# Adding loads for two sums of each weight block, and the down projection's operands kept in DRAM

## The chip, the cores and the metric

The kernel runs on one core of one Trainium2 chip. A time is the device time of one execution in microseconds (us). TensorE (PE) multiplies matrices, with its weight loads (PEld) beside it; VectorE (DVE) and ScalarE (ACT) work elementwise; GpSimd (POOL) does so too and issues DMAs of its own, whose descriptors are made by software; SyncE (SP) issues nearly all other DMAs. Every engine, and every queue of DMA issues, runs its instructions in the order in which the program holds them. An instruction that waits holds up all that stand behind it on its engine.

## What is computed

One layer of a streaming encoder on 576 tokens (512 of a new stream, 64 of a running one): layer norm, a mixer (RWKV-7 and S5), an output projection with a second layer norm, a SwiGLU feed-forward part with a third. The change touches the feed-forward part alone:

```python
def swiglu(x, w1, w3, w2):
    return (jax.nn.silu(x @ w1) * (x @ w3)) @ w2

x = layer_norm(ALPHA * x + mix, ln1_g[l], ln1_b[l])
x = layer_norm(ALPHA * x + swiglu(x, ffn_w1[l], ffn_w3[l], ffn_w2[l]), ln2_g[l], ln2_b[l])
```

The model width is 2048 and the hidden width 5632; all arrays are float32.

## The kernel before

Activations stand transposed: features on the 128 partitions, 576 tokens along the free axis, in two halves of 288. Every float32 operand is split in a high and a low part (`wh`, `wl` for weights), and each product is three matmuls (high-high, high-low, low-high) of 128x128 weights on 128x288 activations.

The feed-forward part multiplies by a Strassen-Winograd scheme. A block pair of weights is a 2x2 arrangement of 128-column blocks of four 128-row tiles each. Seven products do the work of eight, but need sums of blocks: `s1` (product 5), `s2` (product 6), `s3` (product 7), and a changed block for product 3.

`stationary` (L1470) makes the seven weight operands of one call. It loads a raw tile `fr` of 128x8x256 with two DMAs from SP (L1475; the pool `fraw` holds two such tiles), forms `s1` and `s2` on DVE, `s3` (L1484) and the block of product 3 (L1497) on POOL, and for each product casts the high part on ACT (`S.copy(wh, x)`, L1493) and subtracts it on DVE (`wl`, L103). The pool `wsp` has three buffers each for `wh` and `wl`, so at most three products stand ready ahead of PE.

`up` (L1511) is one pair of output blocks of `w1` or `w3`: two calls of `stationary` (q = 0, 1), each followed by 7 x 12 matmuls (`product`, L1505), then eight combinations of the seven PSUM banks into `c` (one copy on ACT, seven additions on DVE through `e` and `f`). The loop over 22 pairs runs `up(w1)`, Silu on ACT, `up(w3)`, the product of both on POOL (L1537) and two stores to the DRAM tensor `gd` (L1538): four calls of `stationary` a pair, 88 in all.

The down projection takes 40 row blocks in five chunks of eight. `moving` (L1554) loads four blocks `g` of a chunk, forms the three sums and the seven operands `gq` from them (DVE, ACT, and POOL in pieces of 128x288), and for each of the eight pairs of output blocks a call of `stationary(w2, ...)` and 7 x 12 matmuls follow (L1614), with results added into `acd` (`fold` on DVE, three additions on POOL). Four row blocks that are left over are done at the end without the scheme.

The order of work is set by a scheduler: `high_priority(offset=250)` around `stationary`, `offset=600` around `moving`. It places instructions by a modelled time, and what it wrote down is then fixed for each engine.

Of the kernel before, what the change touches and what calls it, by code (L numbers as in the profile page):

```python
# [8 lines left out]
F32 = mybir.dt.float32  # L9
# [3 lines left out]
ALU = mybir.AluOpType  # L13
# [4 lines left out]
P = 128  # L18
# [42 lines left out]
def tile_hybrid_step(ctx: ExitStack, tc: tile.TileContext, a, o, dbg=None):  # L61
# [1346 lines left out]
    rps = stats.rstd(pv)  # L1410
    mean = stats.mean()
# [14 lines left out]
    for kh in range(2):  # L1426
        ks = slice(4 * kh, 4 * kh + 4)

        def norm(j, h):
            q = acc[j][:, h, ks]  # L1430
            ts = slice(h * HF, (h + 1) * HF)
            tt(q, q, bcm(mean[:, ts], 4), ALU.subtract)
            tt(q, q, bcm(rstd[:, ts], 4), ALU.mult)
            for k in range(4):
                m = 8 * j + 4 * kh + k
                S.activation(q[:, k], q[:, k], AF.Identity, bias=par["ln1_b"][:, m:m + 1],
                             scale=par["ln1_g"][:, m:m + 1])
# [9 lines left out]
        tt(b11, b12, b11, ALU.subtract)  # L1447
# [19 lines left out]
    def bank(n=HF):  # L1467
        return pd.tile([P, 512], F32, tag="pb", name="pb")[:, :n]

    def stationary(src, r1, r2, col, order):  # L1470


        raw = fraw.tile([P, 8, 256], F32, tag="fr", name="fr")
        for i, r in enumerate((r1, r2)):
            nc.sync.dma_start(raw[:, 4 * i:4 * i + 4], src[r:r + 512, col:col + 256].rearrange("(k p) c -> p k c", p=P))  # L1475
        blk = {(i, j): raw[:, 4 * j:4 * j + 4, i * P:i * P + P] for i in range(2) for j in range(2)}

        def s_(nm):
            return wraw.tile([P, 512], F32, tag="raw", name=nm).rearrange("p (k c) -> p k c", c=P)

        ops, out = {1: blk[0, 0], 2: blk[0, 1], 4: blk[1, 1]}, {}
        s1, s2, s3 = s_("s1"), s_("s2"), s_("s3")
# [3 lines left out]
        ops[5], ops[6], ops[7] = s1, s2, s3  # L1486
# [12 lines left out]

    def product(ps, w, x, first, last):  # L1500
# [10 lines left out]
    def up(src, col):  # L1511

        ps = {n_: bank() for n_ in UP}
        for q in range(2):
            with tc.high_priority(offset=250):
                ws = stationary(src, 512 * q, 1024 + 512 * q, col, UP)
# [15 lines left out]
    for m in range(0, DFF // P, 2):
        sg = up(w1, m * P)
        for x in sg:
            S.activation(x, x, AF.Silu)
# [9 lines left out]
    def operand():  # L1545
# [5 lines left out]
        place.append(room[-1][:, n % 2])  # L1551
        return place[-1]

    def moving(ck):  # L1554

        g = big2.tile([P, 2, 2, 4, HF], F32, tag="big2", name="g")
        for j in range(2):
            r0 = (8 * ck + 4 * j) * P
            for h in range(2):
                nc.sync.dma_start(g[:, j, h], gd[r0:r0 + 4 * P, h * HF:h * HF + HF].rearrange("(k p) n -> p k n", p=P))  # L1560
        b = {(j, h): g[:, j, h] for j in range(2) for h in range(2)}
        out = {}

        def sp(n_, q):
# [4 lines left out]
        sp(1, b[0, 0])  # L1569
        sp(2, b[1, 0])  # L1570
        tt(b[0, 0], b[0, 1], b[0, 0], ALU.subtract)
        t2 = t2_("t2"), t2_("t2")
        t2 = [x for t_ in t2 for x in hs(t_)]
        for k in range(4):
            G.tensor_tensor(t2[k], b[1, 1][:, k], b[0, 0][:, k], ALU.subtract)
        out[6] = operand()
        for k in range(4):
            S.copy(out[6][:, 0, k], t2[k])
            tt(out[6][:, 1, k], t2[k], out[6][:, 0, k].bitcast(F32), ALU.subtract)
            G.tensor_tensor(b[1, 0][:, k], b[1, 0][:, k], t2[k], ALU.subtract)  # L1580
        sp(5, b[0, 0])
        tt(b[0, 1], b[1, 1], b[0, 1], ALU.subtract)
        sp(7, b[0, 1])
        sp(3, b[1, 1])
        sp(4, b[1, 0])
# [6 lines left out]
    def fold(d_, ps, ck):  # L1592
        if ck == 0:
            stt(d_, d_, ALPHA, ps, ALU.mult, ALU.add)
        else:
            tt(d_, ps, d_, ALU.add)

    for ck in range(NCK):
        with tc.high_priority(offset=600):
            gq = moving(ck)  # L1600
        for m in range(0, 16, 2):
            with tc.high_priority(offset=250):
                ws = stationary(w2, 1024 * ck, 1024 * ck + 512, m * P, DOWN)
            c1, c2 = (hs(acc[m // 8][:, m % 8 + i]) for i in range(2))
            pa, pb_, pc = bank(), bank(), bank()
            e, f = hs(w5("e")), hs(w5("f"))
            for n_ in DOWN:
                ps, first, last = {1: (pa, True, False), 2: (pb_, True, True), 6: (pa, False, False), 5: (pc, True, False),
                                   7: (pa, False, False), 3: (pc, False, True), 4: (pa, False, True)}[n_]
                x = gq[n_]  # L1610
                n = 0
                for k in range(4):
                    for w_, x_ in ((ws[n_][0], x[:, 0]), (ws[n_][0], x[:, 1]), (ws[n_][1], x[:, 0])):
                        T.matmul(ps, w_[:, k], x_[:, k], start=first and n == 0, stop=n == 11, skip_group_check=True)  # L1614
                        n += 1
                if n_ == 1:
                    S.copy(e[0], pa)
                elif n_ == 2:
                    fold(c1[0], pb_, ck)
                    G.tensor_tensor(c1[0], c1[0], e[0], ALU.add)  # L1620
                elif n_ == 6:
                    S.copy(e[1], pa)
                elif n_ == 5:
                    fold(c2[1], pc, ck)
                elif n_ == 7:
                    S.copy(f[0], pa)
                    G.tensor_tensor(c2[1], c2[1], f[0], ALU.add)
                elif n_ == 3:
                    fold(c1[1], pc, ck)
                    G.tensor_tensor(c1[1], c1[1], e[1], ALU.add)  # L1630
                else:
                    fold(c2[0], pa, ck)


    NB = 4
# [93 lines left out]
```

## Time and profile before

| | |
|---|---|
| median of 3 runs | 2833.76 us (2829.86 to 2834.14) |
| the profiled execution | 2835.99 us |
| its span, first to last instruction | 2834.1 us |
| PE busy | 2648.2 us (93%) |
| DVE busy | 2177.8 us (77%) |
| ACT busy | 1286.4 us (45%) |
| POOL busy | 683.3 us (24%) |
| DMA, mean | 119 GB/s |
| up part, first to last matmul of L1505 | 1165.5 to 2203.6 us |
| down part, five chunks, L1614 | 2203.9 to 2745.1 us |

Times in the trace count from the first instruction. A PE that is busy is not PE at its peak, since matmuls overlap; how fast they follow each other is read from the starts in the timeline. A row of the timeline has start, duration, engine, line, operation, operands, count, and in brackets how long the engine had been idle and what ended that.

### The profile page before, as it was taken

The page shows a single profiled execution, that of the slowest core. Times are in us where ns is not written, and L with a number is a line of the kernel's source. Part 1 is how long each engine was busy: PE and PEld are TensorE (multiplying, and loading weights), DVE is VectorE, ACT ScalarE, POOL GpSimd, SP SyncE. Part 2 cuts the span into 40 slices and gives each one's busy share as a digit, 9 for nine tenths or more (in the row PEclk, how much of TensorE's full clock was granted, in tenths as well). Part 3 has the DMA queues.
Part 4 walks back from the last instruction along what each step waited for, and adds up shares of the span by engine and source line. Part 5 has one row for each costly group of instructions (what it writes and reads, how often), then busy time and mean ns, then how long its engine had stood idle before and what let it go on. Part 6 is the DMA issues. An engine that isn't in the chain of part 4 may idle for free. (4 is left out here: it accounts for less than half of the span.)

```text
span 2834.1 us, 55090 instructions
## 1 busy us (share of the span) xinstructions
PE 2648.2 (93%) x21280; PEld 2511.0 (89%) x21280; DVE 2177.8 (77%) x4011; ACT 1286.4 (45%) x2535; POOL 683.3 (24%) x609
## 2 busy tenths in 40 slices
PE   6999999999999999499999999999999799899896
PEld 4999998888788889399999999999999788799895
DVE  5768856768786456877777777777777998988888
ACT  5344434455665432544444444444434443444443
POOL 0010000000000000033232333323332656554530
PEclk8999999999999999699999999999999899999998
DMA  6456756433434352233333333333333432332334
GB/s 189 131 134 197 216 174 179 119 99 98 126 78 116 93 152 71 82 132 107 98 107 103 115 104 102 106 99 111 109 105 102 167 108 90 100 117 90 117 99 137
DMA packets 422908, 338.50 MB, mean 119 GB/s; under 512 B 87362, under 2 KB 388532, under 8 KB 421556
## 3 DMA queue, kind: packets, MB, share of 16 engines
q1 hardware_dynamic: 421940, 332.80, 38.5%
q8 instruction: 167, 2.74, 0.4%
q10 hardware_dynamic: 288, 2.10, 0.2%
q14 instruction: 97, 0.79, 0.1%
q0 software_dynamic: 416, 0.07, 0.0%
HBM read 271.11 MB, written 63.79 MB: 118 GB/s over the span
## 5 line engine op out<-in xcount | busy, mean ns | idle before, releaser
L1505 PE MATMUL pb<-xq,wh 128*128 128x288 f32 x4928 | 994.1, 297 | 23.0 <-ACT xq L1417 16.0
L1505 PEld LDWEIGHTS pb<-xq,wh 128*128 128x128 f32 x4928 | 795.1, 189 | 25.4 <-ACT xq L1417 17.3
L1505 PE MATMUL pb<-xq,wl 128*128 128x288 f32 x2464 | 730.7, 297 | 18.5 <-DVE wl L103 18.1
L1493 ACT CAST wh<-fr 128x512 fp32r<-128x512 f32 x512 | 317.7, 621 | 518.1 <-PE pb L1505 338.3
L1614 PE MATMUL pb<-gq,wh 128*128 128x288 f32 x2240 | 462.3, 304 | 36.0 <-DVE acd L103 12.0
L1505 PEld LDWEIGHTS pb<-xq,wl 128*128 128x128 f32 x2464 | 467.0, 190 | 25.3 <-DVE wl L103 25.3
L103 DVE TENSOR_TENSOR wl<-s,wh 128x512 fp32r<-128x512 f32 x384 | 421.5, 1105 | 49.6 <-ACT wh L1493 43.9
L103 DVE TENSOR_TENSOR wl<-fr,wh 128x512 fp32r<-128x512 f32 x512 | 362.2, 715 | 74.9 <-ACT wh L1493 68.3
L1614 PEld LDWEIGHTS pb<-gq,wh 128*128 128x128 f32 x2240 | 368.2, 195 | 47.0 <-DVE acd L103 12.3
L1493 ACT CAST wh<-s 128x512 fp32r<-128x512 f32 x384 | 238.4, 621 | 330.5 <-PE pb L1505 165.3
L1614 PE MATMUL pb<-gq,wl 128*128 128x288 f32 x1120 | 330.8, 306 | 19.2 <-DVE wl L103 18.2
L129 PE MATMUL pb<-xh,wh 128*128 128x288 f32 x1120 | 338.4, 304 | 2.9 <-ACT pbuf L366 2.1
L129 PE MATMUL pb<-xl,wh 128*128 128x288 f32 x1120 | 338.9, 304 | 0.0
L129 PE MATMUL pb<-xh,wl 128*128 128x288 f32 x1120 | 338.0, 304 | 0.5 <-DVE wl L103 0.5
L1484 POOL TENSOR_TENSOR s<-fr 128x512 f32<-128x512 f32 x128 | 185.6, 1450 | 466.9 <-DVE wl L103 448.8
L103 DVE TENSOR_TENSOR wl<-raw,wh 128x512 fp32r<-128x512 f32 x252 | 173.6, 689 | 134.9 <-ACT wh L301 132.6
L301 ACT CAST wh<-raw 128x512 fp32r<-128x512 f32 x252 | 156.2, 620 | 242.7 <-PE pb L129 184.1
L1497 POOL TENSOR_TENSOR fr<-fr,s 128x512 f32<-128x512 f32 x128 | 172.3, 1346 | 370.7 <-DVE wl L103 370.7
L1614 PEld LDWEIGHTS pb<-gq,wl 128*128 128x128 f32 x1120 | 214.7, 195 | 26.8 <-DVE wl L103 26.6
L129 PEld LDWEIGHTS pb<-xh,wh 128*128 128x128 f32 x1120 | 212.4, 190 | 9.3 <-ACT pbuf L366 2.5
L129 PEld LDWEIGHTS pb<-xh,wl 128*128 128x128 f32 x1120 | 211.8, 190 | 7.9 <-DVE wl L103 1.4
L129 PEld LDWEIGHTS pb<-xl,wh 128*128 128x128 f32 x1120 | 212.5, 190 | 4.8 <-issue 0.2
(498 smaller groups left out, 4200.4 us busy)
## 6 DMA issues: line engine op xcount, KB each, us to landing
fr<-in_ffn_w_dram SPq DMA_DIRECT2D x256, 512.0 KB
raw<-in_w_in_dram SPq DMA_DIRECT2D x140, 256.0 KB
raw<-in_w_out_dram SPq DMA_DIRECT2D x64, 256.0 KB
gd<-c SPq DMA_DIRECT2D x44, 288.0 KB
g<-gd SPq DMA_DIRECT2D x20, 576.0 KB
raw<-in_ffn_w_dram SPq DMA_DIRECT2D x32, 256.0 KB
lwd<-low SPq DMA_DIRECT2D x24, 288.0 KB
rkd<-psh SPq DMA_DIRECT2D x24, 288.0 KB
```

Source lines behind the costliest of these rows:

```text
L103: V.tensor_tensor(out, x, y, op)
L129: T.matmul(out, w, x, **kw)
L301: S.copy(wh, raw)
L1484: G.tensor_tensor(s3, blk[0, 0], blk[1, 0], ALU.subtract)
L1493: S.copy(wh, x)
L1497: G.tensor_tensor(blk[0, 1], blk[0, 1], s2, ALU.subtract)
L1505: T.matmul(ps, w_[:, k], x_[:, k], start=first and n == 0, stop=last and n == 11)
L1614: T.matmul(ps, w_[:, k], x_[:, k], start=first and n == 0, stop=n == 11, skip_group_check=True)
```

## The change

**Loads.** `stationary` no longer has one raw tile. It has four, each with two buffers: `a11` and `a2` (both blocks of the second row half in one tile) are plain loads, and `s1` and `s3` are made in two steps: a plain load of one block from SP, and a second load from POOL's queue that adds another block to what stands in the tile (`accum_op=ALU.add`). `s2` and the block of product 3 stay sums of two tiles, both now on DVE. Signs are turned so that the two loaded sums are additions; the operands of the activations, Silu and the folds carry the signs.

**Product of the two halves.** The two gate products move from POOL to DVE.

**Down operands.** For 20 of 22 pairs DVE forms four more tiles of 128x288 (`n1`, `t3`, `n2`, `n4`), and seven stores a pair go to a DRAM tensor `gp`, in place of two to `gd`. `moving` loads each operand ready-made into a quarter of one staging tile `stg` and only splits it.

```diff
-    def stationary(src, r1, r2, col, order):
-        raw = fraw.tile([P, 8, 256], F32, tag="fr", name="fr")
-        for i, r in enumerate((r1, r2)):
-            nc.sync.dma_start(raw[:, 4 * i:4 * i + 4], src[r:r + 512, col:col + 256].rearrange("(k p) c -> p k c", p=P))
...
-        tt(s1, blk[1, 0], blk[1, 1], ALU.add)
-        G.tensor_tensor(s3, blk[0, 0], blk[1, 0], ALU.subtract)
-        tt(s2, s1, blk[0, 0], ALU.subtract)
+    def stationary(halves, col, order):
+        def rows(i, j, n=1):
+            return halves[j][:, :, col + i * P:col + (i + n) * P]
+        def t_(nm):
+            return fraw.tile([P, 4, P], F32, tag=nm, name=nm)
+        a11, s1, s3 = t_("a11"), t_("s1"), t_("s3")
+        a2 = fraw.tile([P, 4, 2 * P], F32, tag="a2", name="a2")
+        nc.sync.dma_start(a11, rows(0, 0))
+        nc.sync.dma_start(s1, rows(1, 0))
+        nc.sync.dma_start(s3, rows(0, 0))
+        nc.gpsimd.dma_start(s1, rows(1, 1), accum_op=ALU.add)
+        nc.gpsimd.dma_start(s3, rows(1, 0), accum_op=ALU.add)
+        nc.sync.dma_start(a2, rows(0, 1, 2))
...
         for n_ in order:
-            if n_ == 3:
-                ops[3] = blk[0, 1]
+            if n_ == 6:
+                tt(s2, s1, a11, ALU.add)
+                tt(a12, a12, s2, ALU.add)
...
-            if n_ == 2:
-                G.tensor_tensor(blk[0, 1], blk[0, 1], s2, ALU.subtract)
...
-        for i, (x, y) in enumerate(zip(sg, up(w3, m * P))):
-            G.tensor_tensor(y, x, y, ALU.mult)
-            nc.sync.dma_start(gd[(m + i) * P:(m + i + 1) * P], y)
+        g = up(w3, 2 * i * P)
+        tt(g[0], sg[0], g[0], ALU.mult)
+        stt(g[1], g[1], -1.0, sg[1], ALU.mult, ALU.mult)
...
+        tt(n1, b11, b12, ALU.subtract)
+        tt(t3, b22, b12, ALU.subtract)
+        stt(n2, n1, -1.0, b22, ALU.mult, ALU.subtract)
+        stt(n4, n2, -1.0, b21, ALU.mult, ALU.subtract)
+        for n_, x in ((1, b11), (2, b21), (3, b22), (4, n4), (5, n1), (6, n2), (7, t3)):
+            nc.sync.dma_start(gp[i, n_], x)
...
     def moving(ck):
...
+        for n_ in DOWN:
+            q = stg[:, len(place) % 4]
+            nc.sync.dma_start(q, gp[4 * ck:4 * ck + 4, n_].rearrange("k p n -> p k n"))
             out[n_] = operand()
```

DVE in the up part, before: the sums of one call. Names: `fr` is the raw tile, `s_18443` and `s_18565` are `s1` of two calls that follow each other, `s_18566` is `s2` of the second.

```order
L103 TENSOR_TENSOR wl<-s_18443,wh 128x512
L103 TENSOR_TENSOR s_18565<-fr 128x512
L103 TENSOR_TENSOR wl<-s_18444,wh 128x512
L103 TENSOR_TENSOR wl<-s_18445,wh 128x512
L103 TENSOR_TENSOR s_18566<-s_18565,fr 128x512
L103 TENSOR_TENSOR wl<-fr,wh 128x512 x4
L103 TENSOR_TENSOR wl<-s_18565,wh 128x512
```

Here `s1` of the next call is formed between products 5 and 6 of this one, and `s2` after product 7.

The same place now. Call A has `a_18317` as its `a2`; call B has `a_18439` (`a11`), `s_18440` (`s1`), `s_18449` (`s2`), `s_18441` (`s3`), `a_18442` (`a2`); `s_18595` and `s_18720` are `s2` of the calls C and D behind B, formed from their `s1` (`s_18586`, `s_18711`) and `a11`.

```order
L103 TENSOR_TENSOR wl<-a_18317,wh 128x512
L103 TENSOR_TENSOR s_18595<-s_18586,a_18585 128x512
L103 TENSOR_TENSOR wl<-a_18439,wh 128x512
L103 TENSOR_TENSOR wl<-a_18442,wh 128x512
L103 TENSOR_TENSOR a_18442<-a_18442,s_18449 128x4x128
L103 TENSOR_TENSOR wl<-s_18440,wh 128x512
L103 TENSOR_TENSOR wl<-s_18449,wh 128x512
L103 TENSOR_TENSOR c_18564<-pb,e 128x288
L103 TENSOR_TENSOR wl<-s_18441,wh 128x512
L103 TENSOR_TENSOR wl<-a_18442,wh 128x512
L103 TENSOR_TENSOR s_18720<-s_18711,a_18710 128x512
L103 TENSOR_TENSOR e<-pb,e 128x288
```

`s2` of C stands ahead of all splits of B, and `s2` of D ahead of the last split of B: each a whole call ahead of the product that uses it.

SP in the up part, before: eight raw loads and two stores a pair.

```order
L1538 DMA gd<-c_18152 128x576
L1538 DMA gd<-c_18153 128x576
L1475 DMA fr<-in_ffn_w_dram 128x4x256 x8
L1538 DMA gd<-c_18684 128x576
L1538 DMA gd<-c_18685 128x576
```

The same now, from `s1` of B (L1484) to `a2` of C (L1488); `s_18587` is `s3` of C.

```order
L1484 DMA s_18440<-in_ffn_w_dram 128x4x128
L1485 DMA s_18441<-in_ffn_w_dram 128x4x128
L1488 DMA a_18442<-in_ffn_w_dram 128x4x256
L1483 DMA a_18585<-in_ffn_w_dram 128x4x128
L1557 DMA gp<-c_18280 128x288
L1557 DMA gp<-n_18294 128x288
L1484 DMA s_18586<-in_ffn_w_dram 128x4x128
L1557 DMA gp<-c_18281 128x288 x2
L1557 DMA gp<-n_18294 128x288
L1485 DMA s_18587<-in_ffn_w_dram 128x4x128
L1557 DMA gp<-n_18295 128x288 x2
L1488 DMA a_18588<-in_ffn_w_dram 128x4x256
```

Four loads a call instead of two, and in every fourth call seven stores among them; the adding loads stand on POOL's queue, which holds nothing else in the up part now.

DVE at a chunk boundary of the down part, before: splits of the operands `gq` and a sum in `g`; the operand that POOL forms in pieces `t` is split at another place nearby.

```order
L103 TENSOR_TENSOR gq<-g,gq 128x1152
L103 TENSOR_TENSOR s_28001<-fr 128x512
L103 TENSOR_TENSOR gq<-g,gq 128x1152
L103 TENSOR_TENSOR wl<-fr,wh 128x512
L103 TENSOR_TENSOR acd_26680<-pb,acd_26680 128x288
L103 TENSOR_TENSOR g<-g 128x1152
L103 TENSOR_TENSOR wl<-fr,wh 128x512
L103 TENSOR_TENSOR s_28002<-s_28001,fr 128x512
```

And now:

```order
L103 TENSOR_TENSOR wl<-s_28177,wh 128x512
L103 TENSOR_TENSOR gq<-stg,gq 128x1152 x2
L106 SCALAR_TENSOR_TENSOR acd_27167<-acd_27167,pb 128x288
L103 TENSOR_TENSOR wl<-a_28178,wh 128x512 x2
L103 TENSOR_TENSOR s_28489<-s_28480,a_28479 128x512
L103 TENSOR_TENSOR gq<-stg,gq 128x1152 x2
L103 TENSOR_TENSOR wl<-a_28339,wh 128x512
```

The sums in `g` (and the pieces `t`) are gone; seven splits of one size are left, from `stg`.

## Rows read from the trace of the kernel before

**Rows 1.** Windows, up and down part: length; busy us (count) per engine; clock; DMA.

```profile
1250.00:2203.60 953.60, 937.17 (x6979) 930.86 (x6978) 738.21 (x1040) 401.47 (x666) 301.70 (x207) 1.00 0.33 108
2203.60:2745.10 541.50, 486.24 (x3364) 467.57 (x3363) 475.13 (x583) 248.59 (x454) 310.56 (x241) 0.95 0.32 106
```

**Rows 2.** Timeline of PE in the up part: a steady stretch and two stalls.

```profile
1748.33 0.43 PE L1505 MATMUL pb<-xq,wh 128*128 128x288 f32 x2
...
1748.73 0.42 PE L1505 MATMUL pb<-xq,wh 128*128 128x288 f32 x2
1749.71 0.40 PE L1505 MATMUL pb<-xq,wl 128*128 128x288 f32 x1 [0.55 <-DVE wl L103]
...
1795.43 0.40 PE L1505 MATMUL pb<-xq,wl 128*128 128x288 f32 x1 [0.66 <-DVE wl L103]
```

**Rows 3.** Waits, 1250 to 2200 us: engine and line, waited for, us, times, longest.

```profile
PE pb L1505 <- DVE wl L103: 16.1, 23, 1.5
...
ACT wh L1493 <- PE pb L1505: 473.3, 486, 2.7
```

**Rows 4.** Groups by line, 1250 to 2250 us: count, busy us, mean ns, idle before.

```profile
L103 DVE TENSOR_TENSOR wl<-s,wh 128x512 fp32r<-128x512 f32 x255 | 274.0, 1084 | 43.5 <-ACT wh L1493 40.1
L103 DVE TENSOR_TENSOR wl<-fr,wh 128x512 fp32r<-128x512 f32 x339 | 231.1, 688 | 65.2 <-ACT wh L1493 60.9
...
L103 DVE TENSOR_TENSOR s<-s,fr 128x512 f32<-128x512 f32 x85 | 95.4, 1122 | 2.9
...
L103 DVE TENSOR_TENSOR s<-fr 128x512 f32<-128x512 f32 x85 | 60.5, 712 | 59.3 <-DMA fr<-in_ffn_w_dram 58.7
L103 DVE TENSOR_TENSOR c<-pb,f 128x288 f32<-128x288 f32 x126 | 55.8, 452 | 39.3 <-POOL c L1537 26.6 <-PE pb L1505 12.6
```

**Rows 5.** Timeline of the first loads from POOL's queue (4 to 8 KB each).

```profile
1.28 0.68 POOL L175 DMA_DIRECT2D nat<-in_ln_in_g_dram  x1 [0.81 <-POOLq L1717]
1.95 0.49 POOL L175 DMA_DIRECT2D nat<-in_ln_in_b_dram  x1
...
7.18 0.50 POOL L175 DMA_DIRECT2D nat<-in_gn_b_dram  x1 [1.76 <-DMA nat<-in_ln_in_g_dram]
8.45 0.50 POOL L175 DMA_DIRECT2D nat<-in_s_d_dram  x1 [0.78 <-DMA nat<-in_ln_in_b_dram]
9.09 0.51 POOL L175 DMA_DIRECT2D nat<-in_glu_b_dram  x1
```

**Rows 6.** Timelines of SP and ACT: a plain 256 KB load and its reader.

```profile
2796.53 0.37 SPq L298 DMA_DIRECT2D raw<-in_ffn_w_dram  x1
...
2799.37 0.62 ACT L301 CAST wh<-raw 128x512 fp32r<-128x512 f32 x1 [3.89 <-DMA raw<-in_ffn_w_dram]
```

**Rows 7.** DMA: packets and share of 16 engines, 2765 to 2800, then 1300 to 2200 us.

```profile
q1 hardware_dynamic: 7966, 3.96, 38.9%
...
q1 hardware_dynamic: 89121, 94.45, 32.0%
```

**Rows 8.** Down part, groups by line, 2260 to 2720 us, columns as in Rows 4.

```profile
L103 DVE TENSOR_TENSOR wl<-s,wh 128x512 fp32r<-128x512 f32 x105 | 122.5, 1170 | 2.0
L103 DVE TENSOR_TENSOR wl<-fr,wh 128x512 fp32r<-128x512 f32 x142 | 110.0, 786 | 6.0 <-ACT wh L1493 4.1
...
L103 DVE TENSOR_TENSOR gq<-g,gq 128x1152 fp32r<-128x1152 f32 x21 | 34.7, 1667 | 0.5 <-ACT gq L1566 0.5
...
L103 DVE TENSOR_TENSOR g<-g 128x1152 f32<-128x1152 f32 x6 | 10.6, 1768 | 0.0
```

**Rows 9.** What PE and PEld sat idle for before L1614: us, times.

```profile
  DVE wl L103: 44.8, 48
  DVE acd L103: 24.3, 33
  DVE gq L103: 18.5, 8
  ACT wh L1493: 17.3, 17
```

More of the change, by code (lines that the diff above doesn't have):

```diff
@@ L1468, in bank @@
         return pd.tile([P, 512], F32, tag="pb", name="pb")[:, :n]
-    def stationary(src, r1, r2, col, order):
-        raw = fraw.tile([P, 8, 256], F32, tag="fr", name="fr")
-        for i, r in enumerate((r1, r2)):
-            nc.sync.dma_start(raw[:, 4 * i:4 * i + 4], src[r:r + 512, col:col + 256].rearrange("(k p) c -> p k c", p=P))
[L1476 to L1482, printed above, removed]
-        tt(s1, blk[1, 0], blk[1, 1], ALU.add)
-        G.tensor_tensor(s3, blk[0, 0], blk[1, 0], ALU.subtract)
-        tt(s2, s1, blk[0, 0], ALU.subtract)
-        ops[5], ops[6], ops[7] = s1, s2, s3
+    def stationary(halves, col, order):
[11 more added lines that the diff above has]
+        nc.sync.dma_start(a2, rows(0, 1, 2))
+        a12, a22 = a2[:, :, :P], a2[:, :, P:]
+        s2 = wraw.tile([P, 512], F32, tag="raw", name="s2").rearrange("p (k c) -> p k c", c=P)
+        ops, out = {1: a11, 2: a12, 3: a12, 4: a22, 5: s1, 6: s2, 7: s3}, {}
         for n_ in order:
-            if n_ == 3:
-                ops[3] = blk[0, 1]
+            if n_ == 6:
+                tt(s2, s1, a11, ALU.add)
+                tt(a12, a12, s2, ALU.add)
             x = ops[n_]
@@ L1515, in up @@
             with tc.high_priority(offset=250):
-                ws = stationary(src, 512 * q, 1024 + 512 * q, col, UP)
+                ws = stationary([src[r:r + 512].rearrange("(k p) c -> p k c", p=P) for r in (512 * q, 1024 + 512 * q)],
+                                col, UP)
             for n_ in UP:
@@ L1530, in up @@
         return c
[L1532 to L1535, printed above, removed]
-        for i, (x, y) in enumerate(zip(sg, up(w3, m * P))):
-            G.tensor_tensor(y, x, y, ALU.mult)
-            nc.sync.dma_start(gd[(m + i) * P:(m + i + 1) * P], y)
+    for i in range(DFF // P // 2):
+        sg = up(w1, 2 * i * P)
+        for x, sign in zip(sg, (1.0, -1.0)):
+            S.activation(x, x, AF.Silu, scale=sign)
+        g = up(w3, 2 * i * P)
+        tt(g[0], sg[0], g[0], ALU.mult)
+        stt(g[1], g[1], -1.0, sg[1], ALU.mult, ALU.mult)
+        if i >= 20:
+            for k in range(2):
+                r0 = (2 * (i - 20) + k) * P
+                nc.sync.dma_start(gd[r0:r0 + P], g[k])
+            continue
+        (b11, b12), (b21, b22) = hs(g[0]), hs(g[1])
+        n1, t3 = hs(w5("n1"))
+        n2, n4 = hs(w5("n2"))
+        tt(n1, b11, b12, ALU.subtract)
[4 more added lines that the diff above has]
+            nc.sync.dma_start(gp[i, n_], x)
     DOWN = (1, 2, 6, 5, 7, 3, 4)
@@ L1552, in operand @@
         return place[-1]
+    stg = big2.tile([P, 4, 4, HF], F32, tag="big2", name="stg")
     def moving(ck):
[L1556 to L1561, printed above, removed]
         out = {}
-        def sp(n_, q):
+        for n_ in DOWN:
+            q = stg[:, len(place) % 4]
+            nc.sync.dma_start(q, gp[4 * ck:4 * ck + 4, n_].rearrange("k p n -> p k n"))
             out[n_] = operand()
@@ L1567, in sp @@
             tt(out[n_][:, 1], q, out[n_][:, 0].bitcast(F32), ALU.subtract)
[L1569 to L1585, printed above, removed]
         return out
@@ L1590, in tile_hybrid_step, with fold @@
         nc.sync.dma_start(acc[i], x1d[1024 * i:1024 * i + 1024].rearrange("(k p) n -> p k n", p=P))
-    def fold(d_, ps, ck):
+    def fold(d_, ps, ck, op):
         if ck == 0:
-            stt(d_, d_, ALPHA, ps, ALU.mult, ALU.add)
+            stt(d_, d_, ALPHA, ps, ALU.mult, op)
         else:
-            tt(d_, ps, d_, ALU.add)
+            tt(d_, d_, ps, op)
     for ck in range(NCK):
@@ L1618, in tile_hybrid_step @@
                 elif n_ == 2:
-                    fold(c1[0], pb_, ck)
+                    fold(c1[0], pb_, ck, ALU.add)
                     G.tensor_tensor(c1[0], c1[0], e[0], ALU.add)
@@ L1623, in tile_hybrid_step @@
                 elif n_ == 5:
-                    fold(c2[1], pc, ck)
+                    fold(c2[1], pc, ck, ALU.subtract)
                 elif n_ == 7:
                     S.copy(f[0], pa)
-                    G.tensor_tensor(c2[1], c2[1], f[0], ALU.add)
+                    G.tensor_tensor(c2[1], c2[1], f[0], ALU.subtract)
                 elif n_ == 3:
-                    fold(c1[1], pc, ck)
+                    fold(c1[1], pc, ck, ALU.add)
                     G.tensor_tensor(c1[1], c1[1], e[1], ALU.add)
                 else:
-                    fold(c2[0], pa, ck)
+                    fold(c2[0], pa, ck, ALU.subtract)
     NB = 4
```

13 lines of the change are left out of this document (7 added, 6 removed).

## Prediction

> **What bounds the kernel now.** I read the stretches first, then what PE waits for in each, then the single groups. In the steady up part (953.6 us) PE runs at full granted clock and is busy 937 us, while DVE is busy 738, ACT 401 and POOL 302 us [rows 1]. In the timeline three matmuls follow each other in 0.40 us, so one takes 133.3 ns; a call of 84 takes 11.2 us and a pair of four calls 44.8 us [rows 2]. The stalls that are left are short: two of them, a pair apart, are 45.7 us apart, so a stall costs about 0.9 us a pair [rows 2], and all waits of PE there sum to 16.1 us [rows 3]. PE bounds this part and little can be won: at most some 20 us. ACT spends 473 us there waiting for PE to free a weight buffer [rows 3]: what lies upstream idles behind PE.
>
> The down part is different. Its 3360 matmuls would take 448 us at 133.3 ns, and it takes 541.5 us [rows 1]: 93 us are lost. DVE is busy 475 of 541 us there [rows 1], and the waits named for PE and its weight loads are for DVE and ACT: splits, folds, operands [rows 9]. Those rows count both halves of PE, so about half their sum, 52 us, is time. The granted clock is 0.95 [rows 1], which means that part of the stretch ran at 1.2 instead of 2.4 GHz: 5% of 541 us, 27 us.
>
> **The change part by part.** Matmuls, ACT casts and weight operands stay as many, so nothing is taken from PE's own work.
>
> DVE in the up part. Two of the three operands s, and all sums on POOL, go. Splits of `s` take 1084 ns against 688 for `fr`, and the second sum 1122 against 712 for the first [rows 4]; I read the longer ones as running beside POOL. Without POOL's sums I price each 128x512 operation at 0.69 us: three splits and one sum a call give back 3 x 0.40 + 0.43 = 1.6 us, 142 us over 88 calls. Added are two gate products a pair, 0.69 x 576/512 = 0.78 us each, and up to four operations of 128x288 at 0.45 us (price of `c<-pb,f` [rows 4]): 3.4 us a pair, 74 us in all. The sum s1 becomes a load, the sum for product 3 comes from POOL to DVE: even. DVE gets lighter and had 215 us idle. Beside PE this is worth what PE waits for DVE: up to 16 us.
>
> DMA traffic. A call now loads 1536 rows of 512 B, 512 of 1 KB, and adds 1024 of 512 B. A packet of 512 B takes 0.389 x 16 x 35 us / 7966 = 27.3 ns, and one of 1 KB about 0.32 x 16 x 900 / 89121 = 51.7 ns [rows 7]. With an adding packet between one and two plain ones that is (41.9 + 26.5 + 28 to 56) / 16 = 6.0 to 7.8 us of all engines a call, against 11.2. The seven stores a pair add under 1 us a call. Hidden, as long as an adding packet stays under some 95 ns. SP issues 23 DMAs a pair at 0.37 us [rows 6], 8.5 of 45 us: hidden.
>
> **The latency of `s1`.** This is the term that decides. Tile `s1` of call C can be loaded only when the split for product 5 of call A, two calls before, has read its buffer. Then come the plain load, the adding load, and `s2` of C on DVE, which the fixed order puts ahead of all splits of B. While DVE waits there, B's splits wait behind it, so PE runs dry; and the next load of this kind waits for the split 5 of B. That is a loop: two calls cannot take less than 2L plus DVE's work between, where L is plain load plus adding load. From the order, from `s2` of C to split 5 of B: five operations of 0.69, 3.45 us. From `s2` of D to split 5 of C: six of 0.69 and six of 0.45, 6.84 us, in the other half of the pairs 0.78 + 0.45 more, mean 7.45. So two calls take at least 2L + 10.9 us, against 22.4 by PE and 22.8 measured. **No loss needs L under 5.75 us.**
>
> The plain load is in the trace: issued at 2796.53, used at 2799.37, 2.84 us for the same 256 KB in rows of 512 B [rows 6]. The adding load is not. The nearest rows are the loads from POOL's queue at the start: the first was issued at 1.28 and ended a wait at 7.18, 5.9 us for 8 KB [rows 5]. Against it as a price: it is the first use of that path, beside large loads, so a warm one may be quicker; it moves 16 rows and not 512, and does not read its target, so the adding one may be slower. From below I bound it by the plain load itself, 2.84 us; from above, the second 16-row load let the queue go on 1.27 us behind the first, the next one, of 8 rows, 0.64 us later [rows 5]; were that difference a price per row (79 ns), 512 rows would take 40 us. But issuing 8 rows and 16 takes the same 0.5 us, which speaks against it. I take the first row and add the data, 512 x 27.3 ns / 16 = 0.87: 6.8 us. Then L = 2.84 + 6.77 = 9.6 us, two calls take 30.1 instead of 22.8, and 43 such twos (the first loads come long before) cost 43 x 7.3 = **+314 us**.
>
> The Trainium skill, "DMA: Bandwidth & Descriptors", section "Anatomy of one DMA — SWDGE (gpsimd) path", gives a load from POOL's queue a fixed 2.0 us plus its bytes at 436 GB/s, an estimate of 2.6 us for 256 KB; by it L would be 5.4 us, the loop would cost nothing, and the time would be that of rival (a). The first rows of that queue, at 5.9 us for 8 KB, do not bear it out.
>
> In the down part the order puts `s2` mostly right ahead of its own call's splits, a call later than in the up part, so two calls have room for an L of about 17 us. POOL's three additions a call stay and stand among the adding loads; I see no loop in that.
>
> **The down part.** Per call DVE gives back 3 x 0.48 + 4 x 0.1 us on splits and 0.5 on the sum [rows 8], some 2.3 of 11.2 us; a chunk boundary loses the two sums in `g` at 1.77 us [rows 8] and POOL's chain of pieces, while seven splits of 1.67 us stay. I take half of the 93 us as regained, **-50 us**, clock included; bounds: -85 (nothing lost but the seven splits at the first chunk) and +20 (POOL, busy making descriptors, holds up its additions). Entry of the up part and the last stage: unchanged, 0.
>
> Sum against the profiled execution's own 2836.0 us (2834.1 of span; 2.2 above the median of the runs): 2836 + 314 - 50 = **3100 us**.
>
> **The rivals.** (a) *The adding load is nearly as quick as a plain one.* For it: the path would be warm, and nothing else is on POOL in the up part. Then the loop hides behind PE and the kernel is faster: 2836 - 17 - 50 = 2769 us. It decides from a landing of 3.7 us on: there L = 6.5 and the loop eats the 50 us of the down part. (b) *Software descriptors or the adding itself bound it.* If an adding load takes 12 us to land, L = 14.8, two calls take 40.6 us and the time is 2836 + 765 - 50 = 3550 us; with 40 us it would be many ms. (c) *DMA engines saturate:* an adding packet of 150 ns makes (41.9 + 26.5 + 154) / 16 = 13.9 us a call, 2836 + 128 x 2.5 - 50 = 3110 us by that alone, near the forecast with another cause. (d) *The sums leave DVE, but DVE is no relief,* because making descriptors slows it as POOL's sums did: then 16 us less are won, inside every range.
>
> **How the numbers follow.** A landing of 4.5 to 9 us (L 7.3 to 11.8) gives 2906 to 3293 us: 0.56, with (c) in it. Over that, (b): 0.20. Landing of 3.7 to 4.5 us, a small loss: 0.07. (a) with a gain: 0.14. Within 0.2%, which is about what a measurement of this kernel can tell from no change: 0.03. The range 2780 to 3500 leaves out the lower half of (a) and the larger part of (b), under 0.2 together. Faster 0.14, same 0.03, slower 0.83.
>
> **What would show it.** Right: in the up part DVE waits ahead of `s2` for the DMA into `s1`, once a call, PE stalls of 3 to 4 us behind it, and two calls take about 30 us; POOL's issue rows for adding loads are short against their landing. (a) shows as PE stalls under 1 us a pair and landings under 3.7 us; (b) as POOL rows of several us each with one right behind another; (c) as a DMA share near 1. The down part should lose its waits for `gq` and run above 0.95 of the clock. What makes the prediction wrong is the one price that no row shows, the landing of an adding load.

## The result, and the profile after

The changed kernel takes 3129.96 us (median of four runs, 3126.05 to 3137.33) against 2832.2 us of the kernel before on the same chip: 1.106 times, interval 1.103 to 1.108, 298 us slower. Forecast were 3100. The profiled execution has a span of 3128.9 us; I read it against the 2834.1 us of before.

Where the 295 us of span stand is read from the first and last matmul of each part. The entry ends 8 us later. The up part, from the first matmul of L1509 to its last, takes 1265.3 us instead of 1038.4: +227 (forecast +314). The gap to the next part grows by 2 us. The down part takes 599.7 us instead of 541.5: +58 (forecast -50). What follows is equal. So the sum came out close because two terms missed in opposite directions, by 87 and by 108 us. That the total lies within some 30 us of the forecast is luck, and both misses have to be explained.

The windows of the changed kernel, up and down part (length; busy us and count of PE, weight loads, DVE, ACT, POOL; granted clock; DMA share; GB/s), answer to [rows 1], though its row of the up part begins 85 us later, in the steady stretch; the whole up part of before has a clock of 0.99:

```profile
1173.00:2438.00 1265.00, 1074.44 (x7389) 1052.06 (x7390) 715.59 (x1240) 446.44 (x742) 223.66 (x174) 0.93 0.68 151
2441.00:3040.00 599.00, 497.50 (x3361) 484.70 (x3361) 368.45 (x561) 245.51 (x437) 226.99 (x197) 0.92 0.70 160
```

No engine is full: PE is idle for 190 us of the up part, DVE is busy for 57% of it, and the DMA engines for 0.68. When no engine is full and the time grows, look for a chain of waits. The page gives its name: the chain of work (shares by engine, then by line), and the row of the sum `s2`, with its idle time:

```profile
PE 46%; DMA 29%; DVE 15%; issue 6%; ACT 2%; SPq 1%; DVEq 0%; POOLq 0%; POOL 0%; ACTq 0%
DMA s<-in_ffn_w_dram 26%; PE pb L129 21%; PE pb L1509 11%; DVE wl L103 7%; PE pb L1612 3%; PE fj L129 2%; PE ch L129 1%; PE pb L1649 1%; PE fi L129 1%; PE st L129 1%; DVE s L103 1%; DMA stg<-gp 1%; PE py L129 1%; DVE a L103 1%; DVE gq L103 1%
...
L103 DVE TENSOR_TENSOR s<-s,a 128x512 f32<-128x512 f32 x128 | 88.9, 695 | 515.1 <-DMA s<-in_ffn_w_dram 515.1
```

All 128 sums `s2` take 89 us, and DVE stands still for 515 us ahead of them, for a load into `s`. The waits of the up part, 1250 to 2400 us (engine and line, waited for, us, times, longest), answer to [rows 3]:

```profile
ACT wh L1499 <- PE pb L1509: 682.4, 512, 8.2
...
DVE s L103 <- DMA s<-in_ffn_w_dram: 341.5, 81, 8.1
...
PE pb L1509 <- DVE wl L103: 166.3, 72, 5.9
```

PE's wait for splits went from 16.1 us to 166.3, in stalls of up to 5.9 us, and ahead of each of them stands a wait of DVE before `s2`: all 72 end within 1.8 us of the start of an `s2` that had waited. One turn of the ring in the timelines of DVE, SP, POOL and PE (start us, us, instruction, idle time before it and who ended it), drawn together, other rows left out:

```profile
1604.24 0.69 DVE L103 TENSOR_TENSOR s<-s,a 128x512 f32<-128x512 f32 x1 [7.57 <-DMA s<-in_ffn_w_dram]
1605.58 0.61 PE L1509 MATMUL pb<-xq,wl 128*128 128x288 f32 x1 [5.38 <-DVE wl L103]
1606.78 0.68 DVE L103 TENSOR_TENSOR wl<-s,wh 128x512 fp32r<-128x512 f32 x1
1607.49 0.37 SPq L1484 DMA_DIRECT2D s<-in_ffn_w_dram  x1
1611.01 1.30 POOL L1486 DMA_DIRECT2D s<-in_ffn_w_dram  x1 [11.17 <-DMA s<-in_ffn_w_dram]
1617.65 0.69 DVE L103 TENSOR_TENSOR s<-s,a 128x512 f32<-128x512 f32 x1 [3.85 <-DMA s<-in_ffn_w_dram]
...
1622.98 0.68 DVE L103 TENSOR_TENSOR wl<-s,wh 128x512 fp32r<-128x512 f32 x1
1623.69 0.37 SPq L1484 DMA_DIRECT2D s<-in_ffn_w_dram  x1
1627.14 1.28 POOL L1486 DMA_DIRECT2D s<-in_ffn_w_dram  x1 [7.19 <-DVE wl L103]
...
1632.09 0.69 DVE L103 TENSOR_TENSOR s<-s,a 128x512 f32<-128x512 f32 x1 [1.98 <-DMA s<-in_ffn_w_dram]
```

Follow it: `s2` runs at 1604.24, and the fourth operation behind it, the split for product 5 at 1606.78, frees a buffer of `s1`. At 1607.49, when it ends, SP issues the plain load, at 1611.01 POOL the adding load, and at 1617.65 the next `s2` has what it waited for. From 1604.24 to 1632.09, two calls, are 27.85 us, where PE needs 22.4. (In the row at 1627.14 the bracket names a split that ended late; by the trace the plain load that POOL waits for landed at 1626.58.) It is the ring of the prediction, with its three members in the order that was forecast. Nor is this turn picked out: in 86 of the 89 calls whose `s2` stands in the up part, `s2` starts 0.02 us after the last completion of its adding load, and from 1250 to 2160 us the plain load is issued 0.03 us after the end of the split that frees its buffer, in all 64 calls.

The down part shows the same ring, where the prediction saw none. Its waits, 2460 to 3035 us:

```profile
DVE s L103 <- DMA s<-in_ffn_w_dram: 157.4, 36, 7.5
POOL acd L1618 <- DVE acd L103: 111.4, 30, 6.4
...
PE pb L1612 <- DVE wl L103: 89.3, 42, 7.3
```

36 of the 39 sums `s2` there start right behind the landing, too. What PE and its weight loads sat idle for before L1612 (us, times), answers to [rows 9]:

```profile
  DVE wl L103: 188.9, 86
  ACT gq L1582: 17.3, 6
  DVE gq L103: 5.1, 4
...
  DVE acd L103: 1.7, 3
```

The waits for DVE's part of `gq` and for `acd`, 18.5 and 24.3 us before, have fallen to 5.1 and 1.7 us as expected, and those for splits rose from 44.8 to 188.9 us. But the waits for `gq` are not lost, as the prediction had it: those for ACT's part of the operands rose from 7.7 us (4.6 and 3.1, on two lines) to 17.3, so that both together went from 26.2 to 22.4 us.

### The profile page after: what moved, and what is told of

It is laid out like the page before. It is cut to its first block, busy times and chain, and to the rows that moved or that the text cites. A ratio compares the mean times of both kernels' runs of the same rounds, so it can differ in the third digit from the quotient of the medians.

```text
span 3128.9 us, 56201 instructions
## 1 busy us (share of the span) xinstructions
PE 2733.2 (87%) x21280; PEld 2587.8 (83%) x21280; DVE 1977.6 (63%) x4110; ACT 1280.8 (41%) x2520; POOL 507.5 (16%) x525
## 4 chain that ended last, share of the span: by engine, by line
PE 46%; DMA 29%; DVE 15%; issue 6%; ACT 2%; SPq 1%; DVEq 0%; POOLq 0%; POOL 0%; ACTq 0%
DMA s<-in_ffn_w_dram 26%; PE pb L129 21%; PE pb L1509 11%; DVE wl L103 7%; PE pb L1612 3%; PE fj L129 2%; PE ch L129 1%; PE pb L1649 1%; PE fi L129 1%; PE st L129 1%; DVE s L103 1%; DMA stg<-gp 1%; PE py L129 1%; DVE a L103 1%; DVE gq L103 1%
## 5 line engine op out<-in xcount | busy, mean ns | idle before, releaser
L1509 PE MATMUL pb<-xq,wh 128*128 128x288 f32 x4928 | 1041.4, 307 | 21.1 <-ACT xq L1419 15.3
L1509 PE MATMUL pb<-xq,wl 128*128 128x288 f32 x2464 | 762.1, 311 | 174.9 <-DVE wl L103 174.1
L1509 PEld LDWEIGHTS pb<-xq,wh 128*128 128x128 f32 x4928 | 840.1, 199 | 23.3 <-ACT xq L1419 16.5
L1509 PEld LDWEIGHTS pb<-xq,wl 128*128 128x128 f32 x2464 | 491.5, 200 | 195.2 <-DVE wl L103 195.2
L1499 ACT CAST wh<-a 128x512 fp32r<-128x512 f32 x512 | 317.8, 621 | 480.8 <-PE pb L1509 339.0
L1612 PE MATMUL pb<-gq,wh 128*128 128x288 f32 x2240 | 471.8, 310 | 14.1 <-ACT gq L1582 8.3
L103 DVE TENSOR_TENSOR wl<-a,wh 128x512 fp32r<-128x512 f32 x512 | 352.1, 696 | 127.1 <-ACT wh L1499 126.4
L1612 PE MATMUL pb<-gq,wl 128*128 128x288 f32 x1120 | 344.3, 314 | 89.4 <-DVE wl L103 89.3
L103 DVE TENSOR_TENSOR s<-s,a 128x512 f32<-128x512 f32 x128 | 88.9, 695 | 515.1 <-DMA s<-in_ffn_w_dram 515.1
L1612 PEld LDWEIGHTS pb<-gq,wh 128*128 128x128 f32 x2240 | 383.4, 202 | 17.0 <-ACT gq L1582 9.0
L1486 POOL DMA_DIRECT2D s<-in_ffn_w_dram x128 | 165.1, 1290 | 1077.7 <-DMA s<-in_ffn_w_dram 593.9
L1612 PEld LDWEIGHTS pb<-gq,wl 128*128 128x128 f32 x1120 | 224.2, 203 | 99.6 <-DVE wl L103 99.6
L103 DVE TENSOR_TENSOR wl<-s,wh 128x512 fp32r<-128x512 f32 x384 | 260.8, 687 | 58.4 <-ACT wh L1499 57.3
```

What stands on the lines that cost most here:

```text
L103: V.tensor_tensor(out, x, y, op)
L1486: nc.gpsimd.dma_start(s1, rows(1, 1), accum_op=ALU.add)
```

## The experiments

Two theories stood against each other. **The ring:** the adding load is not dear, but `s2` stands a call early on DVE, and makes everything behind it wait for the plain load, the adding load and the buffer that the former frees. **The load:** adding loads cost the time themselves, through DMA engines, memory or the making of descriptors, wherever `s2` stands; this covers rivals (b) and (c). All ratios are against the kernel before.

### `s2` a call later

```diff
+    s2 = wraw.tile([P, 512], F32, tag="raw", name="s2").rearrange("p (k c) -> p k c", c=P)
     def stationary(halves, col, order):
...
-        s2 = wraw.tile([P, 512], F32, tag="raw", name="s2").rearrange("p (k c) -> p k c", c=P)
```

In the changed kernel `s2` takes the three buffers of its pool `wraw` in turn; here it has one, so `s2` of C cannot be formed before the split for product 6 of B has read it. Between the orders of DVE in the two traces 120 of the 128 sums `s2` have moved, and of the other 3982 operations some 120. DVE's order now, with B's tiles `a2_25581`, `s1_25579` and C's `s1_25724`:

```
L103 TENSOR_TENSOR a2_25581<-a2_25581,s2_14977 128x4x128
L103 TENSOR_TENSOR wl_25597<-s1_25579,wh_25596 128x512
L103 TENSOR_TENSOR wl_25603<-s2_14977,wh_25602 128x512
L103 TENSOR_TENSOR s2_14977<-s1_25724,a11_25723 128x512
```

> The changed kernel with one alteration: s2 is one tile for all calls instead of two that alternate, so the sum s2 of call C can no longer stand ahead of the splits of call B; in the order it now stands right behind the split for product 6 of B. The loads, plain and adding, stay word for word. The loop theory (the wait of s2 for its own call's s1, placed a call early, makes two calls last 27.8 us): now s1 has about a call more to land, L may be some 12 us against 9.3 measured, so the up part falls from 1265 us to 1040 to 1070, the down part loses its stalls behind s2 too (599 us to 520 to 570), and the kernel takes 2790 to 2880 us. The rival theory (the adding loads themselves cost the time, by DMA engines, memory or descriptors): nothing about them is altered, so the up part stays above 1200 us and the kernel at 3080 to 3150 us.

Measured: 2798.67 us, ratio 0.988 (0.986 to 0.990). The up part takes 1011.6 us, less than forecast for it, and the down part 522.9 us. Its windows:

```profile
1171.00:2182.00 1011.00, 991.28 (x7392) 989.38 (x7391) 739.85 (x1242) 451.22 (x740) 223.65 (x174) 0.99 0.86 188
2185.00:2708.00 523.00, 471.69 (x3364) 458.50 (x3365) 420.88 (x562) 245.16 (x438) 220.40 (x197) 0.97 0.81 183
```

The same loads, the same adding, now at 0.86 of the DMA engines because the calls come faster, and PE is busy for 991 of 1011 us. 331 us hang on the place of one sum. Where 86 sums of the up part had waited for the landing, 11 of 89 do now, for 10.8 us together. The theory of the load falls for the up part.

### `s1` in three tiles

```diff
-        a11, s1, s3 = t_("a11"), t_("s1"), t_("s3")
+        a11, s3, s2 = t_("a11"), t_("s3"), t_("s2")
+        s1 = wraw.tile([P, 512], F32, tag="raw", name="s1").rearrange("p (k c) -> p k c", c=P)
```

> The changed kernel with s1 in three tiles instead of two (and s2 in two of another pool): the loads of s1 of call C then wait for the split of s1 three calls before, not two, and s2 of C again stands behind the split for product 6 of B. Loop theory: three calls (33.6 us by PE) must hold L and some DVE work, so nothing waits: up part 1035 to 1065 us, kernel 2780 to 2870 us, no slower than with one tile for s2, and quicker if L at its slow end (8 us of landing and more) still costs there. Rival theory of adding loads that cost by themselves: 3080 to 3150 us.

Measured: 2793.73 us, ratio 0.987 (0.986 to 0.989); up part 1014.1, down part 515.0 us. The up part is below the range again. This run tells more than it was built for, since `s2` does not stand where the expectation has it. With two buffers of its own it may be formed as soon as the split for product 6 of the call two before has read one. Counted along DVE's order in the trace, seven splits a call, it stands behind the split for product 6 or 7 of that call (86 of 88 calls of the up part). In the changed kernel it stands one to three splits later, ahead of the last split of that call or right behind it. So `s2` is here even earlier than in the changed kernel, the loads are the same, and nothing is lost: only 2 of 90 sums of the up part wait for the landing. What differs is the buffer. With three tiles of `s1`, two calls must hold one L and not two. An early `s2` thus does no harm by itself; it does with two tiles of `s1`.

In both of these kernels what follows the down part takes 3 us longer, 91.7 and 91.4 us instead of 88.5; why was not looked into.

### The ring with a smaller L

The next two keep `s2` early, with two tiles of `s1`, and change L, the time from the plain load to the landing of the second. Both leave out the adding: the second load overwrites `s1`. In the first the orders of all engines in the trace are those of the changed kernel; in the second `s2` stands one operation earlier once in four calls of the up part, and a few operations of the down part have other places.

```diff
-        nc.gpsimd.dma_start(s1, rows(1, 1), accum_op=ALU.add)
+        nc.gpsimd.dma_start(s1, rows(1, 1))
```

> The changed kernel with the second load of s1 still issued from POOL's queue behind the first one, but without adding: it overwrites s1, so the sum of the two blocks is left out of s1, s2 and the operand of products 2 and 3. Same queue, same 512 rows of 512 B, same waits, same order. It tells whether the landing of 5.0 us of that load is the price of the queue or of the adding. If of the queue: landing 4.5 to 5 us, two calls still near 28 us, up part 1220 to 1270 us, kernel 3050 to 3130 us. If of the adding: landing 3 to 4 us, L 6.5 to 7.5, two calls 23 to 24.5 us, up part 1030 to 1090 us, kernel 2800 to 2900 us. I hold the queue for the likelier.

```diff
-        nc.gpsimd.dma_start(s1, rows(1, 1), accum_op=ALU.add)
...
         nc.sync.dma_start(a2, rows(0, 1, 2))
+        nc.sync.dma_start(s1, rows(1, 1))
```

> The changed kernel with the second load of s1 issued plainly from SP's queue, where it overwrites s1 (the adding is left out of s1, s2 and the operand of products 2 and 3); all waits and the place of s2 in the order stay. It changes one number of the loop, L: two plain landings, 3.5 and 3.0 us, make 6.5 instead of 9.3. Loop theory: two calls need 2 x 6.5 + 9.3 = 22.3 us, just under the 23.0 that PE takes where nothing waits: up part 1015 to 1080 us, down part 515 to 560 us, kernel 2790 to 2880 us, with s2 a call early as in the changed kernel. A theory by which the early place of s2 is harmful by itself expects little of it: above 3000 us.

Measured: 2982.06 us, ratio 1.054 (1.051 to 1.057), and 2892.58 us, ratio 1.022 (1.020 to 1.024). Both up parts missed my ranges: 1156.8 us fell between the two cases that I had set for the first, and 1109.7 us is above the 1080 of the second. But L had missed too, and the ring holds the time against L. From the traces, 1250 to 2160 us, means over 64 to 82 calls: the time from the issue of the plain load to that of the second, from there to its last completion, their sum, and the distance of one `s2` to the second next. The column "DVE" is measured by itself: twice the time from the start of an `s2` to the end of the next split for product 5, which frees a buffer.

| second load of `s1` | to second issue | landing | L | two calls | left over 2L | DVE | up part |
|---|---|---|---|---|---|---|---|
| adding, POOL's queue | 3.74 | 5.58 | 9.32 | 28.39 | 9.75 | 9.75 | 1265.3 |
| plain, POOL's queue | 3.83 | 4.11 | 7.94 | 25.80 | 9.9 | 9.75 | 1156.8 |
| plain, SP's queue | 4.09 | 3.06 | 7.15 | 24.69 | 10.4 | 10.28 | 1109.7 |
| adding, `s2` a call later | 5.01 | 5.55 | 10.56 | 22.40 | - | - | 1011.6 |
| adding, three tiles of `s1` | 4.85 | 5.55 | 10.40 | 22.43 | - | - | 1014.1 |

For three sizes of L, what is left over 2L is DVE's work in the ring to within 0.2 us (forecast 10.9). This is the ring, closed: 2L and DVE's work make up the time of two calls, and nothing else has room in it. A cost of the load itself would also come once a call, but it would not vanish in the last two rows, at the same landing and an even longer L. Set against the 22.4 us of PE, L may be (22.4 - 10) / 2 = 6.2 us before it costs anything; this is worked out, no run with the ring has an L so short. The down part goes the same way: with L of 10.1, 9.0 and 7.4 us there (means of 38 calls) it takes 599.7, 568.1 and 520.1 us.

The timelines of SP, POOL and DVE in the kernel without adding show the shorter way, one turn:

```profile
1622.65 0.37 SPq L1484 DMA_DIRECT2D s<-in_ffn_w_dram  x1
1626.08 0.77 POOL L1486 DMA_DIRECT2D s<-in_ffn_w_dram  x1 [7.27 <-DMA s<-in_ffn_w_dram]
1629.71 0.69 DVE L103 TENSOR_TENSOR s<-s,a 128x512 f32<-128x512 f32 x1 [2.92 <-DMA s<-in_ffn_w_dram]
```

3.63 us from issue to use, and a row of 0.77 instead of 1.30 us on POOL. What adding itself costs is not separated from its form: POOL's queue over the whole execution (packets, MB, share of 16 engines), in the changed kernel and with `s1` loaded plainly:

```profile
q0 software_dynamic: 135584, 67.20, 17.5%
```

```profile
q0 software_dynamic: 78240, 67.20, 13.4%
```

The bytes are the same. Without the 416 packets that this queue has in the kernel before as well, 256 adding loads make 528 packets each; the difference over 128 calls leaves 80 for the plain one. Of the 2.5 us by which the adding load lands later than a plain one on SP's queue, the queue thus makes 1.05 and the adding in its form 1.5, if the two simply add up; I had held the queue for the larger share.

### What the rest of the change is worth

```diff
-        a11, s1, s3 = t_("a11"), t_("s1"), t_("s3")
...
+        raw = fraw.tile([P, 8, 256], F32, tag="fr", name="fr")
+        nc.sync.dma_start(raw[:, :4], rows(0, 0, 2))
+        nc.sync.dma_start(raw[:, 4:], rows(0, 1, 2))
...
+        tt(s1, a21, a22, ALU.add)
+        G.tensor_tensor(s3, a11, a21, ALU.add)
...
-                tt(a12, a12, s2, ALU.add)
+                G.tensor_tensor(a12, a12, s2, ALU.add)
```

> Only the loads undone: two plain 512-KB loads a call as in the kernel before, s1 and s2 formed on DVE, s3 and the operand of products 2 and 3 on POOL; the operands of the down projection are still formed in the up part and kept in DRAM. It shows what that half of the change is worth by itself. Loop theory and the theory of costly adding loads alike: up part 1025 to 1050 us, down part 490 to 540 us, kernel 2780 to 2840 us. If the up part stays above 1100 us here, the gate products and stores in the up part are to blame, and both theories fall.

Measured: 2808.32 us, ratio 0.992 (0.990 to 0.994); up part 1038.2, to the microsecond that of before, down part 516.0. So the operands of the down projection, formed early and kept in DRAM, are worth 25 us in the down part; with the gate products, which moved to DVE as well, they cost the up part nothing.

The next kernel takes the same loads and puts the two sums of POOL on DVE as well:

```diff
-        G.tensor_tensor(s3, a11, a21, ALU.add)
+        tt(s3, a11, a21, ALU.add)
...
-                G.tensor_tensor(a12, a12, s2, ALU.add)
+                tt(a12, a12, s2, ALU.add)
```

> No adding load at all: two plain 512-KB loads a call, and all four sums of a call (s1, s2, s3, the operand of products 2 and 3) on DVE, so POOL has none in the up part; down operands formed in the up part as in the changed kernel. Against the kernel with s3 alone by an adding load (2779 us) it tells whether adding loads bring anything. If DVE has room: up part 1015 to 1030 us, down part 495 to 515 us, kernel 2770 to 2800 us, the same as with s3 added in the load. If the fourth sum is too much for DVE in the down part: down part 520 to 545 us, kernel 2800 to 2840 us.

Measured: 2770.56 us, ratio 0.979 (0.977 to 0.980), by its median the quickest of all; up part 1015.1, down part 501.2 us. The two sums give 38 us when they leave POOL, though DVE has two more of them to do. The groups of DVE's splits of `s`, 1250 to 2160 us (count, busy us, mean ns, idle before), first with the sums on POOL, then on DVE, beside the 1084 ns of [rows 4]:

```profile
L103 DVE TENSOR_TENSOR wl<-s,wh 128x512 fp32r<-128x512 f32 x237 | 223.9, 952 | 40.1 <-ACT wh L1501 39.4
```

```profile
L103 DVE TENSOR_TENSOR wl<-s,wh 128x512 fp32r<-128x512 f32 x243 | 166.9, 687 | 20.8 <-ACT wh L1501 20.1
```

With sums on POOL a split of `s` costs 0.26 us more on the mean, three times a call, and the sum `s2` behaves likewise. The Trainium skill, "SBUF — State Buffer", section "SBUF: two separate sides", has the rule for it: a DVE operation with two SBUF inputs and a GpSimd operation that reads SBUF lock each other out of a port pair for a whole instruction. These two rows agree, 952 ns against 687, and the trace shows it split by split: of the splits from 1250 to 2160 us in the former kernel, the 120 that overlap a sum on POOL take 1215 ns on the mean, the other 433 take 684 and none of them more than 693. PE and its weight loads wait 43.6 us for splits in the former up part and 4.4 in the latter. How much of the 38 us is this and how much the later end of POOL's own sums (1454 and 1302 ns each) was not separated.

One more kernel keeps an adding load where no ring is, for `s3` alone:

```diff
-        a11, s1, s3 = t_("a11"), t_("s1"), t_("s3")
+        a11, a21, s3 = t_("a11"), t_("a21"), t_("s3")
...
-        nc.sync.dma_start(s1, rows(1, 0))
+        nc.sync.dma_start(a21, rows(1, 0))
...
-        nc.gpsimd.dma_start(s1, rows(1, 1), accum_op=ALU.add)
...
+        s1 = wraw.tile([P, 512], F32, tag="raw", name="s1").rearrange("p (k c) -> p k c", c=P)
+        tt(s1, a21, a22, ALU.add)
```

> Half of the adding loads undone: s1 is a sum on DVE of two blocks that were loaded plainly; s3, which no operation needs before its own split, is still a plain load and an adding load of 256 KB from POOL's queue. Loop theory: the wait sits with s1 alone, so the loss goes: up part 1035 to 1080 us, kernel 2790 to 2890 us, though DVE has one sum more a call. Rival theory (each adding load costs): one of two is left, about half of the loss: up part about 1150 us, kernel 2950 to 3000 us.

Measured: 2779.18 us, ratio 0.981 (0.980 to 0.983), better than the range; up part 1019.3, down part 500.6 us. Its median is 8.6 us above that of the kernel with all sums on DVE, and the two intervals just overlap, so an adding load in a harmless place brings nothing and costs at most about that. Windows of the two, the one with `s3` added in the load first:

```profile
1163.00:2182.00 1019.00, 997.92 (x7392) 991.62 (x7392) 789.04 (x1328) 449.83 (x741) 111.66 (x87) 0.99 0.67 165
2184.00:2685.00 501.00, 469.00 (x3365) 458.81 (x3366) 430.19 (x601) 245.59 (x439) 174.26 (x159) 0.97 0.67 171
```

```profile
1167.00:2182.00 1015.00, 994.12 (x7390) 991.72 (x7391) 839.17 (x1418) 451.30 (x742) 0.00 (x0) 0.98 0.38 121
2185.00:2686.00 501.00, 472.13 (x3365) 456.22 (x3365) 433.44 (x640) 245.39 (x438) 144.19 (x120) 0.98 0.41 131
```

DVE's fourth sum raises it from 789 to 839 us of a part in which PE is busy 994: it had the room. With one adding load a call the up part took 0.67 of the DMA engines for the result for which plain loads alone take 0.38.

## Why the prediction was right, and where it was not

**The ring of `s1`: right.** It was named with its three members, its place and its condition. PE's stalls behind it are 2.3 us on the mean (166.3 us in 72), where 3 to 4 were forecast. The experiments that move `s2`, give `s1` a third tile or shorten L show that it is the cause in the up part, where it was forecast, and in the down part as well, where it was not.

**Its size: the term of 314 us measured 227.** Three of its numbers were off. The landing of the adding load was taken as 6.77 us and is 5.58; the way from the plain load to the issue of the adding one was taken as 2.84 and is 3.74. These two nearly cancel, L is 9.3 instead of 9.6. DVE's work in the ring was taken as 10.9 and is 9.75: I summed durations of 0.69, but in the turn above four operations start within 2.54 us, 0.635 apart. And the 22.8 us without loss came from a steady stretch, while the whole up part of before is 1038.4 / 44 = 23.6 us for two calls. With the mean of the whole part after, 1265.3 / 44 = 28.76 us, the loss is 44 x (28.76 - 23.60) = 227 us. Of the 87 us, 35 are this baseline, 44 x (23.6 - 22.8); the rest is DVE's work and L. The point from which it costs was put at L = 5.75 us; by the sum above it is nearer 6.2.

**"I see no loop in that": the step that failed.** The prediction says that in the down part the order puts `s2` mostly right ahead of its own call's splits. It does so for two calls near the start. Even the piece of the order that stands ahead of the prediction shows it: `s_28489` is formed, and then come the splits of `a_28339`, the call before. Counted along DVE's order, 32 of the 40 sums `s2` there stand right ahead of all splits of the call before, and five more at least four splits ahead of their own. Further on it looks like this:

```
L103 TENSOR_TENSOR wl_28937<-a2_28902,wh_28936 128x512
L103 TENSOR_TENSOR s2_29189<-s1_29180,a11_29179 128x512
L103 TENSOR_TENSOR wl_29051<-a11_29039,wh_29050 128x512
L103 TENSOR_TENSOR acd1_27167<-acd1_27167,pb_28942 128x288
L103 TENSOR_TENSOR wl_29055<-a2_29042,wh_29054 128x512
```

`s2_29189` stands ahead of the splits of `a11_29039`, a whole call early. The adding load there also stands on POOL behind additions that wait for DVE. In the changed kernel, DVE's sums and POOL's rows in one stretch of the down part:

```profile
2580.50 1.84 POOL L1625 TENSOR_TENSOR acd<-acd,f 128x288 f32<-128x288 f32 x1
2581.27 1.83 POOL L1628 TENSOR_TENSOR acd<-acd,e 128x288 f32<-128x288 f32 x1
2583.50 0.69 DVE L103 TENSOR_TENSOR s<-s,a 128x512 f32<-128x512 f32 x1 [3.62 <-DMA s<-in_ffn_w_dram]
2585.90 1.12 POOL L1618 TENSOR_TENSOR acd<-acd,e 128x288 f32<-128x288 f32 x1 [2.80 <-DVE acd L103]
2589.36 1.30 POOL L1486 DMA_DIRECT2D s<-in_ffn_w_dram  x1 [2.34 <-DMA s<-in_ffn_w_dram]
2594.63 0.69 DVE L103 TENSOR_TENSOR s<-s,a 128x512 f32<-128x512 f32 x1 [5.61 <-DMA s<-in_ffn_w_dram]
2595.97 0.40 PE L1612 MATMUL pb<-gq,wl 128*128 128x288 f32 x1 [3.17 <-DVE wl L103]
```

DVE waits 5.61 us ahead of `s2`, and PE 3.17 behind it. Here POOL's issue itself waits for the plain load; how much the additions in front of it add was not measured by itself, but the way from the plain load to its issue, 4.28 us on the mean against 3.74 in the up part, has a median of 3.56 in both. With `s2` a call later the part falls by 77 us, to 522.9: that is the loop that was left out.

**The -50 of the down part: right in kind, once the ring is away.** The kernels without adding loads of `s1` show it: 541.5 - 501.2 = 40 us with all sums on DVE, 25 of it from the early operands (516.0 with POOL's sums kept), 15 from POOL's sums. With `s2` a call later and both adding loads it is 19 us only. What holds that kernel 22 us behind was not tested by itself, but the trace points at the load: it lands 7.05 us after its issue there on the mean, against 5.55 in its up part, and 29 of 39 sums `s2` wait until it has, for 48.9 us together. With three tiles 20 of 38 wait, for 25.3 us, and the part takes 515.0 us. Why the load lands later there is open.

**DVE's relief: right**, the splits of `s` fell from 1084 to 687 ns, and in the kernels without the ring and without POOL's sums the up part shows 19 to 27 us of gain against the "up to 16" of the text.

**DMA traffic: too cheap, but hidden.** Between 1250 and 2160 us POOL's queue shows (packets, MB, share of 16 engines)

```profile
q0 software_dynamic: 68112, 33.82, 30.4%
```

0.304 x 16 x 910 us / 68112 = 65.0 ns a packet, 2.4 times the 27.3 of a plain one, where "between one and two" was assumed. It stays under the 95 ns from which it would have counted.

**The rivals.** (a) fell at 5.6 us of landing against 3.7 for its point of decision. The Trainium skill's figure, "DMA: Bandwidth & Descriptors", section "Anatomy of one DMA — SWDGE (gpsimd) path", 2.0 us plus bytes at 436 GB/s, an estimate of 2.6 us for this load, is not borne out here: 4.1 us for a plain load on that queue, 5.6 for an adding one. (b) fell with the issue row, 1.30 us for 512 rows. (c) fell as a cause: at a share of 0.86 the up part is quicker than before. (d) fell with the 687 ns: in the changed kernel the 72 splits that overlap a DMA issue of POOL take 690 ns, the others 685.

## What to carry to other kernels

A sum that a load forms saves an engine's operation and puts a chain of two landings in its place; what that costs is decided by where the first reader stands in its engine's fixed order and by which instruction frees the buffer, so draw that ring, count how many turns its buffers allow, and compare the latencies and the work in it with the pace of the bound engine over as many calls (here 2L plus 9.75 us with 22.4), before counting what the engine saves. When an order decides the answer, look at it in the steady state of each part, several calls in, and name the call of every tile. An engine that is off the bound may well be the better place: four sums on DVE beat two of them on POOL by 38 us, and the best kernel with an adding load is no quicker.

## What the runs showed of the hardware

An adding load of 256 KB in rows of 512 B lands 5.6 us after its issue (mean of the up part; 3.06 us for a plain one on SP's queue), takes POOL 1.29 us to issue and 528 packets of 65 ns. PE ran slower when it was fed worse: the granted clock was 0.93 in the up part with stalls of up to 5.9 us, so part of it ran at 1.2 instead of 2.4 GHz, and 0.99 with `s2` a call later, and the same 7392 matmuls kept it busy for 1074 us instead of 991. The longer matmuls are not the cause: over the 64 calls from 1250 to 2160 us DVE is idle for 0.0 us between the start of `s2` and the end of the split for product 5, so the ring of that part does not wait for PE at all.
